# A chunked RWKV-7 recurrence: the chain of states taken one head at a time, or both heads of a pair in one step

## The chip, the core and the metric

The kernel runs on one core of a Trainium2 chip. Its engines work from queues of their own and wait for each other by semaphores: TensorE (PE: matmuls, and PEld, the loading of their weights), VectorE (DVE), ScalarE (ACT), GpSimd (POOL) and SyncE (SP, which starts the DMAs). The metric is the device time of one execution in microseconds (us); less is better.

## The reference, cut to what matters

One decoder layer with 1024 tokens and 1024 channels: attention in three dilated groups, an RWKV-7 mixer with 16 heads of 64 channels, gates that merge the two, an output product and a squared-ReLU MLP. All is float32. The change touches the recurrence of the mixer:

```python
def step(state, inp):                       # per head; state is 64 x 64
    r_t, w_t, k_t, v_t, a_t, b_t = inp
    sa = jnp.einsum('bhvk,bhk->bhv', state, a_t)
    state = (state * w_t[:, :, None, :] + sa[..., None] * b_t[:, :, None, :]
             + v_t[..., None] * k_t[:, :, None, :])
    return state, jnp.einsum('bhvk,bhk->bhv', state, r_t)
_, ys = lax.scan(step, s0, xs)              # over 1024 tokens, from a zero state
```

## The kernel before

The kernel does not scan over tokens. It takes the 16 heads as eight pairs (m = 0 to 7; the heads of a pair lie on partitions 0 to 63 and 64 to 127) and each head's 1024 tokens as 16 chunks of 64. Within a chunk everything is matrix algebra; from chunk to chunk a 64 x 64 state is handed on. For each pair these steps run, each a function: P projects r, k and v out of the hidden rows (`project`, L307: 48 matmuls of 128 x 512 for each of the three, with operands split in a high and a low part); E and F make decays and features (`pair_lora`, `pair_features`, VectorE lines L649 to L709); g forms the products of the features within each chunk, the gram (`pair_gram`: PE L749 in groups of four chunks, each read out by VectorE at L755 and L757); V prepares the values (`pair_values`: PE L722, copies at L726); I inverts 32 unit triangles at once on VectorE (`pair_inverse`: 60 operations at L775 and L777 between two pairs of transposes, L769 and L781); L builds from all this one 128 x 128 matrix for each chunk and head (`pair_local`: PE L816, L820, L838, L853, with ScalarE copies at L817 and L854 and VectorE work at L845, L855 and L858), left in the tiles `fe`; C runs the chain (`pair_chain`); N normalizes (`pair_norm`), and G are gate projections (again L307).

The chain has 16 steps. The tile `sv` holds for each chunk a 128 x 64 operand: rows 0 to 63 are the chunk's values, rows 64 to 127 the state that enters it. PE multiplies it with the chunk's matrix in `fe` (L874); rows 0 to 63 of the product are the chunk's output, rows 64 to 127 the state that leaves it, which VectorE takes out of PSUM, scales by the decay `dd` (one number per row and chunk) and writes into the next chunk's `sv` (L877). Before, each head has its own `sv` tiles and its own PSUM bank (`ch0`, `ch1`, from the pool psC with one buffer each) for eight chunks; after eight chunks ScalarE copies the outputs into `y` (L880), and the next eight chunks use the same two banks. pair_norm uses the banks of psC too (L900, L911).

The string ORDER names the order in which the steps are written: "... P3 G2 C2 E3 F3 N2 g3 I3 V3 L3 P4 G3 C3 ...", so the chain of one pair stands beside projections and features of the next. The instructions are then laid by a scheduler, which takes for each engine what its own prices say is ready first, in the order of writing; the dense matmuls of P and G fill PE where the rest waits. Each engine then works in exactly that order. The gates G7 to G15 stand behind the last chain. The pool psS gives the gram, the values and the local steps two PSUM banks in all, so that each group of the gram (two banks) waits until VectorE has emptied the group ahead of it.

Of the kernel before, what the change touches and what calls it, by code (L numbers as in the profile page):

```python
# [8 lines left out]
F32 = mybir.dt.float32  # L9
# [4 lines left out]
OP = mybir.AluOpType  # L14
# [35 lines left out]
class Block:  # L50
# [608 lines left out]
    def pair_features(self, st, pr, m):  # L659

        nc = self.nc
        f4, b8 = st["f4"], st["b8"]
# [5 lines left out]
        ch = lambda ap: ap.rearrange("p (c t) -> p c t", t=64)  # L668
        ar = b8.tile([128, 2, S], F32, name="ar", bufs=1)
        bk = b8.tile([128, 16, 2, 64], F32, name="b8")  # L670
        dd = f4.tile([128, 2, 16], F32, name="dd", bufs=2)
        sv = [[f4.tile([128, 8, 64], F32, name="sv", bufs=6) for b in range(2)] for h in range(2)]
        pr.update(ar=ar, bk=bk, dd=dd, sv=sv)
        ar4 = ar.rearrange("p a (f c t) -> p (a f) c t", f=2, t=32)
        pr["ar4"] = ar4
# [3 lines left out]
        for i, hs in enumerate(halves):  # L679
            n = bk[:, 8 * i:8 * i + 8, 1, :]  # L680
            nc.scalar.activation(n, ch(k[:, hs]), AF.Square, scale=C("k_k"))
            p = pn[:, hs]
# [5 lines left out]
        for i, hs in enumerate(halves):  # L688
            c8 = slice(8 * i, 8 * i + 8)
# [21 lines left out]
    def pair_values(self, st, pr, m):  # L711


        nc = self.nc
# [3 lines left out]
        for i in range(2):  # L718
            hs = slice(512 * i, 512 * i + 512)
            pv = psS.tile([128, 4, 128], F32, name="s")  # L720
            for q in range(4):
                nc.tensor.matmul(pv[:, q, :], v[:, 512 * i + 128 * q:512 * i + 128 * q + 128], self.center,  # L722
                                 start=True, stop=True)
            for h in range(2):
                for e in range(2):
                    nc.scalar.copy(sv[h][i][0:64, e:8:2, :], pv[64 * e:64 * e + 64, :, 64 * h:64 * h + 64])  # L726
            nc.gpsimd.tensor_tensor(r[:, hs], r[:, hs], k[:, hs], OP.mult)
            p = psS.tile([128, 512], F32, name="s")
            nc.tensor.matmul(p, brk, r[:, hs], start=True, stop=True)
# [131 lines left out]
    def pair_chain(self, st, pr, m):  # L861

        nc = self.nc
        f4 = st["f4"]
        fe, sv, dd = pr["fe"], pr["sv"], pr["dd"]
        y = f4.tile([128, 16, 64], F32, name="lt", bufs=NLT)
        for h in range(2):
            nc.gpsimd.memset(sv[h][0][64:128, 0, :], 0.0)
        for b in range(2):
            ps = [st["psC"].tile([128, 8, 64], F32, name=f"ch{h}") for h in range(2)]  # L870
            for c8 in range(8):
                c = 8 * b + c8
                for h in range(2):
                    nc.tensor.matmul(ps[h][:, c8, :], fe[b][:, h, c8, :], sv[h][b][:, c8, :],  # L874
                                     start=True, stop=True)
                    if c < 15:
                        nc.vector.tensor_scalar(sv[h][(c + 1) // 8][64:128, (c + 1) % 8, :], ps[h][64:128, c8, :],  # L877
                                                dd[64:128, h, c:c + 1], None, op0=OP.mult)
            for h in range(2):
                nc.scalar.copy(y[64 * h:64 * h + 64, 8 * b:8 * b + 8, :], ps[h][0:64])  # L880
        pr["y"] = y

    def pair_norm(self, st, pr, m):
# [528 lines left out]
```

## Time and profile before

| | before |
|---|---|
| median of 3 runs | 2275.87 us (2270.26 to 2278.08) |
| the profiled execution | 2280.91 us |
| its span in the trace | 2279.2 us |
| PE busy | 2090.6 us, 92%, 10002 instructions |
| VectorE busy | 1567.8 us, 69%, 2845 instructions |
| ScalarE busy | 1036.3 us, 45%, 2018 instructions |
| GpSimd busy | 621.9 us, 27%, 461 instructions |

The span is what the trace covers, the execution's own time a little more. A share of busy time is a mean over all stages: attention comes first, the recurrence stands between about 430 and 1340 us, then come the gates, the merge, the output product and the MLP. The profile's chain of the work that ended last covers the later stages, so the recurrence has to be read from the busy time in stretches and from the waits. Where two records of one engine overlap, their durations add to more than its busy time. Times in views are microseconds from the start of the span, unless a duration is marked ns.

### The profile page before, as it was taken

The numbers are of one execution on the slowest core, as the hardware profiler recorded it, in microseconds if no ns is written. First come the engines' busy times: TensorE is split into PE (matmuls) and PEld (weight loads), VectorE is DVE, ScalarE is ACT, GpSimd is POOL, SyncE is SP. The second block draws the span as 40 slices with busy tenths as digits, with TensorE's granted clock in tenths as the row PEclk, the third lists the DMA queues.
The fourth block names the chain that finished last, engine by engine and source line by source line (L and its number), as shares of the span: only waits on it lengthen the run. The fifth ranks groups of instructions, "written<-read, shape, count | busy, mean of one in ns | idle before, by whom it ended". The sixth has DMA issues, their size and how long they took to land. (4 is left out here: it accounts for less than half of the span.)

```text
span 2279.2 us, 28241 instructions
## 1 busy us (share of the span) xinstructions
PE 2090.6 (92%) x10002; PEld 1628.6 (71%) x10002; DVE 1567.8 (69%) x2845; ACT 1036.3 (45%) x2018; POOL 621.9 (27%) x461
## 2 busy tenths in 40 slices
PE   6798999988989989898989999998699999999997
PEld 3676676666777767677777778876467777788876
DVE  5845555468879787867877744428766553799997
ACT  5534433345454635444645442126545443533332
POOL 2504310321213131222222133201000000988860
PEclk9999999999999999998998999999899999999998
DMA  7513311100011110101010164323354333433222
GB/s 257 169 31 102 98 38 33 56 28 24 25 33 37 31 34 29 34 29 34 24 48 31 54 202 144 125 93 118 118 168 161 116 106 125 155 128 114 93 102 74
DMA packets 156315, 194.88 MB, mean 86 GB/s; under 512 B 10729, under 2 KB 110211, under 8 KB 154127
## 3 DMA queue, kind: packets, MB, share of 16 engines
q1 hardware_dynamic: 156175, 193.08, 25.5%
q8 instruction: 79, 1.29, 0.2%
q14 instruction: 61, 0.50, 0.1%
HBM read 152.14 MB, written 40.90 MB: 85 GB/s over the span
## 5 line engine op out<-in xcount | busy, mean ns | idle before, releaser
L307 PE MATMUL d<-hh,w_h 128*128 128x512 f32 x960 | 329.0, 415 | 7.2 <-ACT w_h L64 4.0
L307 PE MATMUL d<-hl,w_h 128*128 128x512 f32 x960 | 331.1, 415 | 2.9 <-DVE hl L280 2.9
L307 PE MATMUL d<-hh,w_l 128*128 128x512 f32 x960 | 324.8, 410 | 2.6 <-DVE w_l L65 2.6
L1108 PE MATMUL m<-op 128*128 128x512 f32 x1272 | 295.8, 394 | 11.5 <-POOL op L65 6.4
L65 POOL TENSOR_TENSOR w_l<-w_t,w_h 128x256 fp32r<-128x256 f32 x160 | 129.3, 810 | 633.6 <-PE d L307 293.4
L1108 PEld LDWEIGHTS m<-op 128*128 128x128 f32 x1272 | 240.0, 190 | 66.9 <-POOL op L65 10.6
L1108 PE MATMUL m<-big,op 128*128 128x512 f32 x1152 | 275.1, 399 | 5.1 <-ACT op L64 2.1
L1108 PEld LDWEIGHTS m<-big,op 128*128 128x128 f32 x1152 | 212.8, 188 | 67.3 <-DVE u L1220 4.2
L64 ACT CAST w_h<-w_t 128x256 fp32r<-128x256 f32 x272 | 108.7, 404 | 316.4 <-PE d L307 230.7
L307 PEld LDWEIGHTS d<-hl,w_h 128*128 128x128 f32 x960 | 181.5, 193 | 45.5 <-issue 10.1
L307 PEld LDWEIGHTS d<-hh,w_h 128*128 128x128 f32 x960 | 180.8, 193 | 46.3 <-issue 5.7
L307 PEld LDWEIGHTS d<-hh,w_l 128*128 128x128 f32 x960 | 181.1, 192 | 44.0 <-issue 8.5
L64 ACT CAST op<-t 128x512 fp32r<-128x512 f32 (+1 forms) x152 | 114.2, 776 | 182.8 <-PE m L1108 121.5
L65 DVE TENSOR_TENSOR op<-t,op 128x512 fp32r<-128x512 f32 (+1 forms) x124 | 118.5, 975 | 28.0 <-ACT op L64 27.8
L153 POOL TENSOR_TENSOR macc<-macc,ada_t 128x512 f32<-128x512 f32 x56 | 87.5, 1564 | 181.3 <-ACT macc L151 162.7
L1266 POOL TENSOR_TENSOR t<-big 128x1024 f32<-128x1024 f32 x7 | 16.9, 2410 | 352.1 <-DMA big<-in_w_ff_dram 331.3
L1282 DVE TENSOR_TENSOR big<-big,m 128x1024 f32<-128x1024 f32 x88 | 104.4, 1210 | 3.8 <-PE m L1108 3.8
L775 DVE TENSOR_TENSOR lt<-lt 64x30 f32<-64x30 f32 (+14 forms) x240 | 96.9, 404 | 8.2
L777 DVE TENSOR_TENSOR lt<-lt 64x30 f32<-64x30 f32 (+14 forms) x240 | 94.2, 392 | 7.7
L874 PEld LDWEIGHTS ch<-sv,fe 128*128 128x128 f32 x512 | 83.3, 191 | 20.3 <-DVE sv L877 8.9
L65 DVE TENSOR_TENSOR w_l<-w_t,w_h 128x256 fp32r<-128x256 f32 x112 | 61.6, 555 | 48.6 <-ACT w_h L64 34.9
L65 POOL TENSOR_TENSOR op<-t,op 128x1024 fp32r<-128x1024 f32 x28 | 93.2, 3339 | 4.3 <-ACT op L64 4.3
(379 smaller groups left out, 3925.8 us busy)
## 6 DMA issues: line engine op xcount, KB each, us to landing
w_t<-in_w_in_dram SPq DMA_DIRECT2D x240, 128.0 KB
ada_t<-in_ada_w_dram SPq DMA_DIRECT2D x64, 256.0 KB
fS<-ft SPq DMA_DIRECT2D x64, 256.0 KB
t<-in_w_ff_dram SPq DMA_DIRECT2D x16, 1024.0 KB
big<-fS SPq DMA_DIRECT2D x16, 1024.0 KB
big<-in_w_ff_dram SPq DMA_DIRECT2D x16, 1024.0 KB
x<-in_x_dram SPq DMA_DIRECT2D x16, 512.0 KB
ada_t<-in_ada_w_dram SPq DMA_DIRECT2D x16, 512.0 KB
```

Source lines behind the costliest of these rows:

```text
L64: nc.scalar.copy(hi, t)
L65: (eng or nc.vector).tensor_tensor(lo, t, hi.bitcast(F32), OP.subtract)
L153: nc.gpsimd.tensor_tensor(acc, acc, t, OP.add)
L307: nc.tensor.matmul(p[:, 512 * half + cs.start:512 * half + cs.stop], a, b[half][k][:, cs], start=k == ks[0] and i == 0, stop=k == ks[-1] a ...
L775: nc.vector.tensor_tensor(q, lb[:, s + 1:32, s:s + 1].to_broadcast([64, n, s]), lb[:, s:s + 1, 0:s].to_broadcast([64, n, s]), OP.mult)
L777: nc.vector.tensor_tensor(lb[:, s + 1:32, 0:s], lb[:, s + 1:32, 0:s], q, OP.add)
L874: nc.tensor.matmul(ps[h][:, c8, :], fe[b][:, h, c8, :], sv[h][b][:, c8, :], start=True, stop=True)
L1108: self.nc.tensor.matmul(p, s, m, start=start and k == 0 and i == 0, stop=k == len(a) - 1 and i == 2, skip_group_check=not start)
L1266: vb.tensor_tensor(sb[:, 0], wr[:, k1, h2], wr[:, k1, h1], OP.subtract)
L1282: nc.vector.tensor_tensor(acc[nm][h], acc[nm][h], ps2[h], OP.add)
```

## The change

Both heads of a pair go through the chain together. One `sv` tile holds both heads for eight chunks. The 16 steps are cut in four quarters; a quarter has one PSUM bank, in which the two heads' products of a chunk lie side by side, and the quarters use the banks `ch0` and `ch1` in turn. VectorE takes both states in one tensor_tensor of 64 partitions by 2 by 64 elements, whose second operand is `dd` read with a step of zero over the 64 columns. The copies into `sv` (pair_values) become two for each half, with 512 elements, the copies into `y` two for each quarter, with 256 elements.

```diff
-        sv = [[f4.tile([128, 8, 64], F32, name="sv", bufs=6) for b in range(2)] for h in range(2)]
+        sv = [f4.tile([128, 2, 8, 64], F32, name="sv", bufs=3) for b in range(2)]
...
-            for h in range(2):
-                for e in range(2):
-                    nc.scalar.copy(sv[h][i][0:64, e:8:2, :], pv[64 * e:64 * e + 64, :, 64 * h:64 * h + 64])
+            for e in range(2):
+                nc.scalar.copy(sv[i][0:64, :, e:8:2, :],
+                               pv[64 * e:64 * e + 64].rearrange("p q (h t) -> p h q t", h=2))
...
-        for h in range(2):
-            nc.gpsimd.memset(sv[h][0][64:128, 0, :], 0.0)
-        for b in range(2):
-            ps = [st["psC"].tile([128, 8, 64], F32, name=f"ch{h}") for h in range(2)]
-            for c8 in range(8):
-                c = 8 * b + c8
+        nc.gpsimd.memset(sv[0][64:128, :, 0, :], 0.0)
+        for q in range(4):
+            ps = st["psC"].tile([128, 4, 2, 64], F32, name=f"ch{q % 2}")
+            for i in range(4):
+                c = 4 * q + i
                 for h in range(2):
-                    nc.tensor.matmul(ps[h][:, c8, :], fe[b][:, h, c8, :], sv[h][b][:, c8, :],
+                    nc.tensor.matmul(ps[:, i, h, :], fe[c // 8][:, h, c % 8, :], sv[c // 8][:, h, c % 8, :],
                                      start=True, stop=True)
-                    if c < 15:
-                        nc.vector.tensor_scalar(sv[h][(c + 1) // 8][64:128, (c + 1) % 8, :], ps[h][64:128, c8, :],
-                                                dd[64:128, h, c:c + 1], None, op0=OP.mult)
+                if c < 15:
+                    nc.vector.tensor_tensor(sv[(c + 1) // 8][64:128, :, (c + 1) % 8, :], ps[64:128, i],
+                                            dd[64:128, :, c:c + 1].to_broadcast([64, 2, 64]), OP.mult)
             for h in range(2):
-                nc.scalar.copy(y[64 * h:64 * h + 64, 8 * b:8 * b + 8, :], ps[h][0:64])
+                nc.scalar.copy(y[64 * h:64 * h + 64, 4 * q:4 * q + 4, :], ps[0:64, :, h, :])
```

The scheduler lays all engines anew. On VectorE, in the chain of pair 1, `sv` are the states (L877, now L876), the other rows the features of pair 2. Before:

```order
L705 TENSOR_TENSOR b8_5612<-rkv_5346,ft_5593 128x8x64
L877 TENSOR_SCALAR sv_4741<-ch0_5507,dd_4739 64x64
L877 TENSOR_SCALAR sv_4743<-ch1_5508,dd_4739 64x64
L707 COPY dd_5613<-ft_5630 64x8 x2
L708 TENSOR_TENSOR ar_5611<-ft_5628,ft_5630 128x2x256
L709 TENSOR_TENSOR ar_5611<-rkv_5270,ft_5630 128x2x256
L877 TENSOR_SCALAR sv_4741<-ch0_5543,dd_4739 64x64
L877 TENSOR_SCALAR sv_4743<-ch1_5544,dd_4739 64x64
L694 SCALAR_TENSOR_TENSOR ft_5644<-rkv_5346,col_166,b8_5612 128x512
```

and now, at the seam of two quarters:

```order
L709 TENSOR_TENSOR ar_5575<-rkv_5246,ft_5608 128x2x256
L876 TENSOR_TENSOR sv_4723<-ch0_5512,dd_4721 64x2x64
L755 TENSOR_TENSOR b8_5667<-s_5670,gmask_160 128x4x2x32
L757 TENSOR_TENSOR fe_5668<-s_5670,gmask_160 128x4x64
L876 TENSOR_TENSOR sv_4723<-ch1_5527,dd_4721 64x2x64
L755 TENSOR_TENSOR b8_5667<-s_5671,gmask_160 128x4x2x32
L757 TENSOR_TENSOR fe_5668<-s_5671,gmask_160 128x4x64
```

Where two updates stood between pieces of the features there is one, and the readings of the next gram (L755, L757) have come into the chain.

On PE, at the end of the same chain (products L874, now L873), L307 are dense matmuls that fill, and L749 are products of the next pair's gram. Before:

```order
L874 MATMUL ch_5544<-sv,fe 128x64
L307 MATMUL d<-hh,w_l 128x512
L307 MATMUL d<-hh,w_h 128x512 x2
L307 MATMUL d<-hl,w_h 128x512 x2
L749 MATMUL s<-ar,b_5612 128x128 x8
L307 MATMUL d<-hh,w_l 128x512 x2
```

and now:

```order
L873 MATMUL ch_5527<-sv,fe 128x64 x2
L749 MATMUL s<-ar,b_5576 128x128 x7
L307 MATMUL d<-hh,w_h 128x512
L749 MATMUL s<-ar,b_5576 128x128 x4
L307 MATMUL d<-hl,w_h 128x512 x2
L307 MATMUL d<-hh,w_l 128x512 x2
```

A group of eight gram products stood behind the chain with five dense matmuls between; now seven products of the gram follow the chain's last step at once, and most of the others stand ahead of it. From the chain's end to the eight L816 of this pair PE has 112 dense matmuls in place of 106 and 15 gram products in place of 24.

On PE behind the chain of a later pair the gram stays whole. In pair 4, before:

```order
L874 MATMUL ch_8166<-sv,fe 128x64
L307 MATMUL d<-hh,w_l 128x512
L307 MATMUL d<-hh,w_h 128x512 x2
L307 MATMUL d<-hl,w_h 128x512 x2
L307 MATMUL d<-hh,w_l 128x512
L749 MATMUL s<-ar,b_8234 128x128 x8
```

and now, in pair 5:

```order
L873 MATMUL ch_8951<-sv,fe 128x64 x2
L307 MATMUL d<-hl,w_h 128x512
L307 MATMUL d<-hh,w_l 128x512 x2
L307 MATMUL d<-hh,w_h 128x512 x2
L749 MATMUL s<-ar,b_9000 128x128 x8
L307 MATMUL d<-hl,w_h 128x512 x2
```

From the first group of eight to the second there are 20 dense matmuls in the one and 21 in the other. In the order before this is so in pairs 2, 4 and 6, in the new one in pairs 3 and 5; in pairs 2, 4 and 6 the new order has one group of eight inside the chain and 19 dense matmuls from the chain's end to the next group.

## Rows read from the trace of the kernel before

**Rows 1.** Stretch, length, busy us of PE, PEld, DVE, ACT, POOL (count); clock, DMA, GB/s.

```profile
538.52:645.67 107.15, 96.07 (x502) 76.49 (x502) 86.89 (x191) 53.85 (x113) 23.07 (x27) 0.91 0.08 25
645.67:742.59 96.92, 87.05 (x493) 69.49 (x493) 82.52 (x187) 53.60 (x110) 22.31 (x28) 0.98 0.10 31
742.59:854.14 111.55, 100.56 (x531) 79.51 (x531) 87.85 (x193) 55.14 (x113) 25.32 (x31) 0.94 0.11 33
854.14:953.82 99.68, 90.20 (x499) 71.21 (x499) 84.35 (x187) 53.66 (x110) 22.85 (x28) 0.96 0.10 32
953.82:1069.86 116.04, 106.30 (x533) 85.11 (x533) 87.11 (x194) 55.53 (x114) 25.06 (x31) 0.88 0.10 32
1069.86:1169.57 99.71, 89.46 (x499) 71.49 (x499) 83.83 (x187) 53.77 (x110) 22.67 (x28) 0.96 0.10 32
1169.57:1278.69 109.12, 99.83 (x517) 80.02 (x517) 83.98 (x188) 53.99 (x114) 24.52 (x29) 0.89 0.14 45
1336.20:1544.80 208.60, 207.08 (x909) 169.85 (x907) 80.49 (x88) 58.19 (x98) 46.02 (x31) 1.00 0.43 137
```

**Rows 2.** Waits of PE, 560 to 1340 us: us in total, times, longest.

```profile
PE s L816 <- ACT lt L817: 31.5, 7, 5.2
PE s L749 <- DVE fe L757: 7.5, 3, 2.5
...
PE ch L874 <- DVE sv L877: 1.5, 4, 0.4
```

**Rows 3.** VectorE in order of time: start, us, line, operation, tiles, shapes, count.

```profile
679.82 0.50 DVE L877 TENSOR_SCALAR sv<-ch,dd 64x64 f32<-64x64 f32 x2
680.34 0.69 DVE L704 SCALAR_TENSOR_TENSOR b<-ft 128x512 f32<-128x512 f32 x1
```

**Rows 4.** PE in order of time, chain and gram (a product shows two records).

```profile
678.79 0.63 PE L307 MATMUL d<-hh,w_l 128*128 128x512 f32 x2
679.25 0.55 PE L874 MATMUL ch<-sv,fe 128*128 128x64 f32 x4
...
680.62 0.55 PE L874 MATMUL ch<-sv,fe 128*128 128x64 f32 x4
...
682.00 0.55 PE L874 MATMUL ch<-sv,fe 128*128 128x64 f32 x4
...
683.83 0.33 PE L874 MATMUL ch<-sv,fe 128*128 128x64 f32 x2
...
696.04 1.71 PE L749 MATMUL s<-ar,b 64*128 64x128 f32 x16
```

**Rows 5.** Groups by line and shape, 560 to 1270 us: busy us, mean ns; idle before.

```profile
L877 DVE TENSOR_SCALAR sv<-ch,dd 64x64 f32<-64x64 f32 x210 | 55.1, 289 | 17.1 <-PE ch L874 14.0
...
L755 DVE TENSOR_TENSOR b<-s,gmask 128x256 f32<-128x256 f32 x56 | 24.4, 435 | 31.2 <-PE s L749 30.8
...
L757 DVE TENSOR_TENSOR fe<-s,gmask 128x256 f32<-128x256 f32 x56 | 23.3, 416 | 0.1
...
L726 ACT COPY sv<-s 64x256 f32<-64x256 f32 x56 | 20.6, 368 | 6.4 <-PE s L722 5.9
...
L880 ACT COPY lt<-ch 64x512 f32<-64x512 f32 x28 | 16.2, 577 | 15.8 <-PE ch L874 10.9 <-DVE sv L877 4.6
...
L709 DVE TENSOR_TENSOR ar<-rkv,ft 128x512 f32<-128x512 f32 x14 | 10.4, 744 | 0.2
...
L840 DVE TENSOR_TENSOR lt<-lt,s 128x512 f32<-128x512 f32 x12 | 8.2, 686 | 3.7 <-PE s L838 3.5
```

**Rows 6.** PE in order of time, at the gram of the fifth period.

```profile
1009.88 0.39 PE L307 MATMUL d<-hh,w_h 128*128 128x512 f32 x1
1012.79 1.13 PE L749 MATMUL s<-ar,b 64*128 64x128 f32 x8 [2.52 <-DVE fe L757]
```

**Rows 7.** Two stretches with a gram, columns as in rows 1.

```profile
900.00:917.00 17.00, 15.97 (x103) 12.94 (x103) 15.68 (x42) 6.48 (x14) 6.64 (x6) 1.00 0.09 25
1012.00:1036.00 24.00, 22.26 (x79) 17.19 (x80) 13.13 (x32) 7.06 (x15) 7.25 (x6) 0.57 0.04 12
```

## The prediction

> **What bounds the kernel now.** I read the stretches first. One period of the recurrence stage, from the end of one pair's triangular inverse on VectorE to the end of the next one's, takes 97 to 116 us [rows 1]. In it the reader should see that no engine is full: PE is busy 87 to 106 us, VectorE 82 to 88 us. PE's idle part is nearly the same in all seven periods: 107.15 - 96.07 = 11.1 us in the first, then 9.9, 11.0, 9.5, 9.7, 10.3 and 9.3 us, together 70.7 us. What differs is the clock: 0.98 in the shortest period, 0.88 in the longest. [...] Behind the stage stands a stretch in which PE is busy 207.08 of 208.60 us at clock 1.00 (the last row of [rows 1]): the gate projections that nothing holds up. So a microsecond that PE loses less in the stage is a microsecond off the end, and matmuls that only change sides cost nothing. [...]
>
> Next the waits of PE [rows 2]. The chain itself hardly holds PE: 1.5 us in all. The largest wait is that of the eight transposes at L816 for the ScalarE copy at L817, 31.5 us over seven, so 4.5 us a pair; L817 waits for the inverse on VectorE, which runs without a gap up to it. The second is the gram at L749, which waits for VectorE to empty a bank (L757): 7.5 us, three times. PE therefore waits for VectorE's queue, not for the chain's latency. VectorE carries the 30 chain operations of a pair in front of both places.
>
> **The change part by part.** *VectorE, 30 operations a pair become 15.* In the trace two L877 in a row take 0.50 us, and the next operation starts 0.52 us after the first [rows 3]; alone one takes 0.289 us [rows 5]. The combined operation, 64 partitions by 128 elements out of PSUM with a second tensor from SBUF, is not in the trace. The nearest are the tensor_tensor of 256 elements out of PSUM (L755, L757, 0.416 and 0.435 us) and of 512 (L840, 0.686 us) [rows 5]: about 1.0 ns an element between them, so an estimate of 0.30 us at 128. Bounds: not below one L877, 0.29 us; at most the price at 256 elements, 0.43 us. With the same 0.03 us behind it a step costs 0.33 us in place of 0.52: 0.19 us by 15 steps is 2.9 us a pair, 23 us over eight. At the dear end it is 0.06 by 120, 7 us. I take 0.30, because the two neighbours lie on a line and the operand read by broadcast is no longer than the mask that L757 reads by broadcast.
>
> The rows price a 64-element operation out of PSUM at 0.289 us and a 256-element one at 0.42 to 0.44 us [rows 5]. [...]
>
> *PE, the same 32 products a pair.* Tiles, shapes and weights are the same; only the bank and the order differ; of the dense matmuls 706 in place of 690 stand behind the last chain, 3.6 us that leave the stage and come back after it. In the trace a step's two products stand behind four dense matmuls, and steps start 1.37 us apart (679.25, 680.62, 682.00), the first two rows giving 0.23 us for a dense matmul [rows 4]. Cost 0.
>
> *The chain's latency.* Before, head 0's update runs while PE does head 1's product; now one update waits for both. A step from rows: two products of 0.23 us each, 0.30 us of VectorE, two hand-overs of about 0.1 us, 0.95 to 1.0 us. The dense matmuls between steps hide that: three or four stand there (0.7 to 0.9 us on top of the 0.46 us of products). Where nothing stands between, in the new order only at a run of six products in pairs 3 and 5, PE idles 0.5 us a step, twice per pair: 2 us in all.
>
> *Banks.* With one bank a head, step 8 had to wait for the copies at L880: it starts 1.83 us after step 7 [rows 4], 0.46 us more than the others. With four banks' worth of steps in two alternating banks a copy has a whole quarter of the chain. That saves at most 0.46 by 8, 3.7 us, and it was covered by dense matmuls, so I book 0.
>
> *ScalarE and GpSimd.* The result copies go from 4 of 512 elements to 8 of 256: 8 by 0.368 - 4 by 0.577, +0.64 us; the value copies go the other way, -0.64 us [rows 5]. Nothing; ScalarE is busy half of a period [rows 1]. Two memsets become one. No DMA and no queue of SP changes.
>
> *What arrives at PE's waits.* The scheduler lays the work anew, so I counted the two orders from the last chain step of a pair to the eight L816, each row at its mean duration. Pair 1 in full: VectorE has 3 L755, 3 L757 and one L709 fewer there, 3 by 0.435 + 3 by 0.416 + 0.744 = 3.3 us, the rest is the same work [rows 5]; PE has nine gram products fewer (a run of eight takes 1.71 us [rows 4], so 1.9 us) and six dense matmuls more (1.4 us), 0.5 us less. VectorE's lead over PE, which is the wait, shrinks by some 2.9 us, from 7.0 to 4.0. The same count for pairs 0 to 6 gives a VectorE excess of 7.0, 7.0, 8.3, 7.0, 8.3, 7.0, 7.4 us before and 4.1, 4.0, 5.8, 7.8, 5.8, 7.8, 6.2 us after: 52 against 41.5, so 10.5 us less idle. Pairs 3 and 5 get worse, since there the chain now ends before the features' second half. PE's own wait for the chain, 1.5 us [rows 2], goes as well, since PE's rows outweigh VectorE's there in the new order. Together 12 us.
>
> *The clock.* PE lost 52 us to the lower clock with 70.7 us of idle time, 0.74 us per microsecond [rows 1]. I carry that ratio: 12 by 1.74 is 20.9 us. With the 2 us of bare steps the **sum is -19 us**. The profiled execution took 2280.91 us, which makes 2262; it lies 5 us above the median of the runs, 2275.87, so for the median **2257 us**. Bounds: without the clock's share 12 - 2 = 10 us, 2266; with all of VectorE's 23 us arriving and the clock's share, 23 by 1.74 = 40 us, 2236; at VectorE's dear end 7 by 1.74 - 2 = 10 us, 2266 again.
>
> **The rivals.** *The whole relief arrives* (2236 us). For it: VectorE is gapless for most of the stretch before L816. It needs pairs 3 and 5 not to lose what the others win, and the gram's stall not to come back. That stall is the trace's clearest slip: in the fifth period PE runs out of dense matmuls at 1010.3 us, waits 2.52 us for L757 [rows 6], and the next 24 us go at clock 0.57, where the same place one period earlier went at 1.00 [rows 7]. Against it: the new order keeps that gap in pairs 3 and 5.
>
> *No difference* (2276 us, 2269 to 2283). The orders are laid by a planner with its own prices. PE waits at L816 because VectorE is later than planned; the chain's saving was planned with, so fewer dense matmuls stand in the chain (43 in place of 53 in pair 1) and the same lateness returns at L816. For it: PE's idle part is 9.3 to 11.1 us in every period, whatever the order in it. The same time comes out if the combined operation costs what two did. Against it: the count above shows a lead shrinking in five of seven pairs.
>
> *Slower, by the gram's slip* (2291 us). Periods with the slip average (111.55 + 116.04 + 109.12) / 3 = 112.2 us, the three without it 98.8 us [rows 1]; the counts of PE's rows differ by 6.8 us (90.1 against 83.3), so a slip costs 6.6 us. Before, it sits in pairs 2, 4 and 6. Counted from the chain's end to the second group of the gram, PE arrives there after 7.5 us and VectorE is done with the first group after 10.2; the new order has the same figures in pairs 3 and 5, and 4.3 against 5.7 us in pairs 2, 4 and 6. If these slip as well there are five in place of three, +13 us, and the bare steps +2, with the relief eaten up at half clock. It decides where PE's wait at that place passes from tenths of a microsecond to over 2 us.
>
> **How the numbers follow.** Forecast 0.48, whole relief 0.17, no difference 0.20, slower 0.15. A measurement of this kernel can tell about 0.3%, 7 us, from no change. Both faster cases lie below 2269: faster 0.65, within 0.20, slower 0.15. The forecast's own range is 2236 to 2268; the range for 8 in 10 reaches from 2234 into the slower case, to 2284, which leaves out some 0.05 below and 0.1 above.
>
> **What would show it.** 120 operations of 64 by 128 elements at 0.29 to 0.33 us (0.43 or more would make it the second rival); VectorE's busy time in a period down by about 3 us; the wait L816 for L817 down from 4.5 to about 3 us a pair, but not in pairs 3 and 5; PE's idle part per period 8 to 9 us; clock 1.00 at the gram of pairs 2, 4 and 6 and below 0.8 at that of 3 and 5. The forecast is wrong if PE's idle part stays at 10 us, if waits for the chain's update (L873 for L876) grow beyond some 5 us, or if the stretch behind the stage stops being full of PE work.

## The result, and the profile after

The changed kernel takes 2294.1 us (median of 4 runs) against 2275.9 us: a ratio of 1.0081, 95% interval 1.0056 to 1.0107. It is **slower** by 0.8%, where 0.8% faster was forecast, and it lies outside the range. The profiled execution took 2289.69 us with a span of 2288.0 us.

First the seven periods and the stretch behind the stage, cut as in [rows 1] (stretch, length, busy us of PE, PEld, DVE, ACT, POOL, clock, DMA, GB/s):

```profile
537.16:639.60 102.44, 90.25 (x499) 71.44 (x499) 80.88 (x177) 53.85 (x112) 22.36 (x25) 0.95 0.09 26
639.60:740.72 101.12, 89.26 (x492) 70.75 (x492) 80.37 (x173) 53.28 (x109) 23.36 (x26) 0.96 0.10 30
740.72:845.15 104.43, 94.05 (x512) 74.12 (x512) 83.08 (x176) 53.92 (x111) 22.30 (x27) 0.97 0.10 32
845.15:958.69 113.54, 101.12 (x519) 78.61 (x519) 83.50 (x176) 55.16 (x113) 24.62 (x29) 0.91 0.10 31
958.69:1065.60 106.91, 96.40 (x513) 74.92 (x513) 83.69 (x175) 54.19 (x112) 22.33 (x27) 0.95 0.10 31
1065.60:1180.15 114.55, 101.65 (x519) 79.17 (x519) 83.48 (x176) 55.14 (x113) 24.62 (x29) 0.89 0.10 31
1180.15:1285.69 105.54, 96.02 (x500) 75.30 (x500) 80.35 (x174) 53.33 (x112) 22.19 (x26) 0.90 0.12 41
1343.80:1552.40 208.60, 207.06 (x909) 170.05 (x909) 79.07 (x83) 58.31 (x97) 45.94 (x32) 1.00 0.43 138
```

See three things. The stretch behind the stage is as full of PE work as before, so what PE loses in the stage still moves the end. VectorE is busy 575.4 us in the seven periods, against 596.5: the 21 us that the change was to save are saved. And PE's idle part is larger all the same: 79.8 us against 70.7. The clock's loss, estimated as (1 - clock) times the length and summed over the seven periods, is 51 us, against 52 from [rows 1]. The fourth and the sixth period, which hold the chains of pairs 3 and 5, went from 99.7 us each to 113.5 and 114.6; the second grew by 4.2 us, and the first, third, fifth and seventh together went from 443.9 to 419.3. Not all of this is loss, since dense matmuls moved between the periods (519 PE records in place of 499 in the fourth and the sixth, 512 and 513 in place of 531 and 533 in the third and the fifth); idle time and the clock's loss together rose by some 20 us in the fourth and sixth and fell by some 12 in the other five.

The waits of PE, 560 to 1340 us (us, times, longest), to hold against [rows 2]:

```profile
PE s L816 <- ACT lt L817: 37.9, 7, 5.7
PE s L749 <- DVE fe L757: 9.3, 9, 2.6
PE ch L899 <- POOL lt L893: 7.2, 6, 1.8
PE ch L873 <- DVE sv L876: 5.1, 12, 0.6
```

The large wait rose by 6.4 us where it was to fall by 10, and the wait for the chain's operation, 1.5 us before, is 5.1. The combined operation itself, by line and shape over 560 to 1270 us (busy us, mean ns, idle before), cost what was estimated:

```profile
L876 DVE TENSOR_TENSOR sv<-ch,dd 64x128 f32<-64x128 f32 x105 | 30.9, 295 | 25.7 <-PE ch L873 23.2
```

0.295 us for 128 elements out of PSUM, where one head's 64 took 0.289 [rows 5].

What happens in the fourth period is seen in order of time (start, us; idle before). The chain of pair 3 now begins when nearly all of its own local work is done and the dense matmuls have run out:

```profile
875.26 0.66 PE L873 MATMUL ch<-sv,fe 128*128 128x64 f32 x4 [0.39 <-DVE sv L876]
875.95 0.29 DVE L876 TENSOR_TENSOR sv<-ch,dd 64x128 f32<-64x128 f32 x1 [0.75 <-PE ch L873]
...
876.30 0.66 PE L873 MATMUL ch<-sv,fe 128*128 128x64 f32 x4 [0.39 <-DVE sv L876]
...
877.00 0.29 DVE L876 TENSOR_TENSOR sv<-ch,dd 64x128 f32<-64x128 f32 x1 [0.75 <-PE ch L873]
...
878.07 1.11 PE L873 MATMUL ch<-sv,fe 128*128 128x64 f32 x4
...
878.94 0.77 PE L645 MATMUL d<-dws,lorah 128*128 128x512 f32 x1
...
879.65 0.79 PE L646 MATMUL d<-dws,loral 64*128 64x512 f32 x1
...
880.37 1.11 PE L873 MATMUL ch<-sv,fe 128*128 128x64 f32 x4
...
904.76 0.39 PE L307 MATMUL d<-hh,w_l 128*128 128x512 f32 x1
...
907.77 4.23 PE L749 MATMUL s<-ar,b 64*128 64x128 f32 x16 [2.62 <-DVE fe L757]
```

A step takes 1.05 us (875.26 to 876.30) with both engines waiting for each other in it. From 878 on the same products take 1.11 us in place of 0.66: the granted clock, 1.00 from 873 to 876 us, is 0.50 from 878 to 886. A step with two products of the lora step in it (L645, L646) takes 2.3 us there. At 907.77 the gram has its slip (PE waits for VectorE to empty a bank), as in the periods of [rows 6] before. Two stretches of this period, the bare part of the chain and the gram, show the clock (0.74 in both):

```profile
873.00:893.00 20.00, 19.23 (x77) 13.29 (x75) 10.02 (x23) 12.75 (x21) 0.79 (x2) 0.74 0.09 33
904.00:917.00 13.00, 10.20 (x46) 7.87 (x45) 10.16 (x28) 1.57 (x3) 4.11 (x5) 0.74 0.05 15
```

### The profile page after: what moved, and what is told of

Read it like the earlier page. It is cut to its first block, busy times and chain, and to the rows that moved or that the text cites. A ratio compares the mean times of both kernels' runs of the same rounds, so it can differ in the third digit from the quotient of the medians.

```text
span 2288.0 us, 28138 instructions
## 1 busy us (share of the span) xinstructions
PE 2094.2 (92%) x10002; PEld 1623.3 (71%) x10002; DVE 1522.1 (67%) x2725; ACT 1037.9 (45%) x2018; POOL 617.9 (27%) x453
## 5 line engine op out<-in xcount | busy, mean ns | idle before, releaser
L307 PE MATMUL d<-hh,w_h 128*128 128x512 f32 x960 | 324.9, 411 | 7.3 <-ACT w_h L64 4.0
L307 PE MATMUL d<-hh,w_l 128*128 128x512 f32 x960 | 323.2, 410 | 3.6 <-DVE w_l L65 3.6
L307 PE MATMUL d<-hl,w_h 128*128 128x512 f32 x960 | 320.4, 408 | 0.0
L307 PEld LDWEIGHTS d<-hh,w_h 128*128 128x128 f32 x960 | 181.1, 193 | 45.7 <-ACT w_h L64 4.8
L307 PEld LDWEIGHTS d<-hh,w_l 128*128 128x128 f32 x960 | 180.9, 192 | 45.7 <-issue 7.6
L307 PEld LDWEIGHTS d<-hl,w_h 128*128 128x128 f32 x960 | 180.1, 191 | 40.5 <-issue 7.4
L64 ACT CAST op<-t 128x512 fp32r<-128x512 f32 (+1 forms) x152 | 113.7, 776 | 172.1 <-PE m L1107 119.6
L775 DVE TENSOR_TENSOR lt<-lt 64x30 f32<-64x30 f32 (+14 forms) x240 | 94.6, 394 | 13.2 <-PE ch L899 2.7
L873 PEld LDWEIGHTS ch<-sv,fe 128*128 128x128 f32 x512 | 74.7, 199 | 28.8 <-DVE sv L876 14.1
L65 DVE TENSOR_TENSOR w_l<-w_t,w_h 128x256 fp32r<-128x256 f32 x112 | 56.3, 506 | 53.6 <-ACT w_h L64 42.4
```

The costliest lines, as they stand in the source:

```text
L64: nc.scalar.copy(hi, t)
L65: (eng or nc.vector).tensor_tensor(lo, t, hi.bitcast(F32), OP.subtract)
L307: nc.tensor.matmul(p[:, 512 * half + cs.start:512 * half + cs.stop], a, b[half][k][:, cs], start=k == ks[0] and i == 0, stop=k == ks[-1] a ...
L775: nc.vector.tensor_tensor(q, lb[:, s + 1:32, s:s + 1].to_broadcast([64, n, s]), lb[:, s:s + 1, 0:s].to_broadcast([64, n, s]), OP.mult)
L873: nc.tensor.matmul(ps[:, i, h, :], fe[c // 8][:, h, c % 8, :], sv[c // 8][:, h, c % 8, :], start=True, stop=True)
```

## The experiments

Two kernels that differ in one operation are laid in two different orders by the planner, so a comparison holds little unless the order is held. Kernel 1 is the kernel of run 1, and so on. Most of them therefore carry a table of the wanted order, engine by engine, and edges that only order (no wait is added between engines):

```diff
+def pin(tc, nc):
...
+    info = mybir.DependencyInfo(mybir.DependencyClass.NoSync, mybir.DependencyReason.SCHED_ONLY)
+    for e, t in TABLE.items():
+        o = array.array("H", zlib.decompress(base64.b85decode(t)))
+        for a, b in zip(o, o[1:]):
+            tc.add_manual_dep(at[e][b], at[e][a].name, info, reason="order")
...
         Block(tc, aps, out).build()
+        pin(tc, nc)
```

All ratios are to the kernel before, on the same chip, with 95% intervals.

### 1 and 2: the instructions of the one in the order of the other

Edit of 1: `pin` with the order of the kernel before, on the changed kernel. Edit of 2: `pin` with the changed kernel's order, on the kernel before.

> All the instructions of the changed kernel, but on each engine in the order of the kernel before: the planner's choice is overruled by edges that only order, the combined operation stands where the second head's operation stood, and 32 of the 64 copies of the chain's results on ScalarE, which have no counterpart, are left to the planner. Nothing is left out of the computation. Theory O (the combined operation and the shared bank cost nothing, the loss is the planner's new order): 2250 to 2266 us, 10 to 26 us under the kernel before (120 operations of 0.29 us fewer is 35 us, 120 x (2 x 0.289 - 0.295) = 34 us of VectorE time at most, 23 by the plain count of busy time after), and the changed kernel's extra idle of TensorE in pairs 3 and 5 gone. Rival L (in lockstep each step has to wait for both products, and that latency is on the path): 2280 to 2300 us in any order, TensorE waiting for the combined operation well over 5 us more than in the kernel before. Rival B (one bank for both heads, four banks in place of two, copies cut otherwise): 2280 to 2300 us too, and then the third run of this call shows it without the combined operation.

> All the instructions of the kernel before, but on each engine in the order of the changed kernel: the two operations of a step stand together where the combined one stood; 64 value copies, 32 result copies on ScalarE and 16 memsets on GpSimd, which have no counterpart, are left to the planner. Nothing is left out of the computation. Theory O: no faster than the changed kernel, 2292 to 2318 us: the stretches of pairs 3 and 5 are as long as there or longer (113 us against 99.7 before), since 23 us of VectorE time come back and the chain is as bare. Rivals L and B: the separate operations and banks bring the time back to that of the kernel before, 2270 to 2282 us.

Measured: 2298.8 us, 1.0107 (1.0080 to 1.0135), and 2303.4 us, 1.0126 (1.0101 to 1.0152). The second is as theory O has it: with not one operation changed, the new order costs 1.3%, and its fourth and sixth period are 115.2 and 113.7 us long, as in the changed kernel. Part of it may be kernel 2's own: PE waits 5.3 us there for ScalarE's copy L880 out of the two banks, a wait that neither the kernel before nor the changed kernel shows. So whether the combined operation gives anything back in that order (the changed kernel, 1.0081) is not shown; the two intervals overlap as well. But the first speaks against theory O: the order of before with the combined operation is as bad. PE's waits in it, 560 to 1340 us:

```profile
PE s L816 <- ACT lt L817: 31.4, 7, 5.3
PE ch L873 <- DVE sv L876: 13.2, 31, 1.1
```

The largest wait is that of [rows 2]. New is that PE stands 31 times at a product whose state isn't there.

### 3 and 4: the shared bank with two operations, and a third order

Edit of 3, on the changed kernel, with `pin` to the order of before:

```diff
-                if c < 15:
-                    nc.vector.tensor_tensor(sv[(c + 1) // 8][64:128, :, (c + 1) % 8, :], ps[64:128, i],
-                                            dd[64:128, :, c:c + 1].to_broadcast([64, 2, 64]), OP.mult)
+                    if c < 15:
+                        nc.vector.tensor_scalar(sv[(c + 1) // 8][64:128, h, (c + 1) % 8, :], ps[64:128, i, h, :],
+                                                dd[64:128, h, c:c + 1], None, op0=OP.mult)
```

Edit of 4: the changed kernel, `pin` with the order that the planner makes of kernel 3 when nothing is pinned.

> The changed kernel's tiles (both heads in one tile of states, one PSUM bank a quarter for both heads, its copies and memsets), but two separate operations a step, one a head, and on each engine the order of the kernel before. Nothing is left out of the computation. Theory O and rival L: as the kernel before, 2270 to 2282 us, VectorE's busy time 1567 us as before. Rival B: 2284 to 2300 us.

> The changed kernel's instructions in a third order: the one that the planner makes of the changed tiles with two operations a step. In it the chain of each of pairs 0 to 6 is written among the next pair's features and all four groups of its gram, so that no gram stands whole behind a chain. Nothing is left out of the computation. Theory O: the stretches of pairs 3 and 5 fall to 95 to 103 us from 113.5 and 114.5, no wait of TensorE for L757 over 1.5 us in pairs 2 to 6, and the time is 2240 to 2268 us. Rivals L and B: no better than the changed kernel, 2285 to 2305 us, since each step's latency stays.

Measured: 2366.5 us, 1.0412 (1.0386 to 1.0438), and 2339.7 us, 1.0279 (1.0253 to 1.0306). Kernel 3, PE's waits and then VectorE's, 560 to 1340 us:

```profile
PE ch L873 <- DVE sv L876: 43.2, 73, 2.3
```

```profile
DVE sv L876 <- PE ch L873: 79.2, 131, 1.6
```

What ran as two chains beside each other is one chain twice as long, and costs 92 us in this order: between 500 and 1290 us 74 of 210 operations overlap a product on PE in the kernel before, one of 206 here. The two heads share a tile of states and a bank. Kernel 7 below, with the shared tile and a bank for each head, has 75 such overlaps and no loss, so the bank is what is left. That is rival B's side, far above its range. Why the product of one head and the operation of the other take turns in the shared bank is not shown; that they do is in the waits above (43.2 us of PE for the operation, 79.2 of VectorE for the product). So the shared bank is not neutral: with the one operation it is free (kernel 5 below), with two in this order it is dear; two operations with the heads in step, as in kernel 6, were not run in it. Kernel 4, slower than any range given for it, refutes theory O's best case: a chain among the features and all of the gram is no remedy. VectorE waits 85.6 us for products there (19.8 before), and the wait at L816 is 53.7 us.

### 5 to 7: both products of a step together, and the tile of states

Edit of 5: kernel 1 with one change to PE's list, made at each of the 128 steps. In rows of PE:

```diff
-L873 MATMUL ch_4641<-sv,fe 128x64
-L307 MATMUL d<-hh,w_h 128x512
-L873 MATMUL ch_4641<-sv,fe 128x64
+L307 MATMUL d<-hh,w_h 128x512
+L873 MATMUL ch_4641<-sv,fe 128x64 x2
```

Edit of 6: the same move in the kernel before, on PE for the products and on VectorE for the two operations. Edit of 7, on the kernel before, nothing pinned: of the change only the one tile `sv` for both heads, with its copies and its one memset.

> As the first run of this study (the changed kernel's instructions in the order of the kernel before), with one difference: the first head's product of each step is moved down to stand directly ahead of the second head's, so that TensorE no longer comes early to a product whose state isn't there. Nothing is left out of the computation. In the first run TensorE waited 13.2 us for the combined operation (1.5 us for L877 in the kernel before) and VectorE 62.8 us for the products (19.8). Theory S (stagger: the two heads' chains of the kernel before run out of phase, so that one's product is made while VectorE updates the other; the combined operation puts them in phase, and the two engines wait for each other in turn): still 2275 to 2300 us, VectorE's wait for the products over 30 us. Rival P (only the early place of the first head's product costs): 2250 to 2270 us, TensorE's wait for the operation under 4 us and VectorE's for the products about 20 us.

> The kernel before with its two operations a step and its two banks, and with its own order but for the chain: both products of a step stand together in the place of the second, and both operations in the place of the second. Nothing is left out of the computation. It has the phase of the combined operation without the operation. Theory S: 2285 to 2310 us, VectorE's wait for the products over 30 us (19.8 before). Rival P, and any theory in which the shared bank or the combined operation itself costs: 2270 to 2282 us.

> One part of the change alone: the states of both heads in one tile, with its half as many value copies of twice the size and its one memset; two banks, two operations a step, copies of the results as before. Nothing is left out of the computation. Theory S and rival P: as the kernel before, 2270 to 2282 us. Rival B (the tile of states or its copies cost): 2284 us or more.

Measured: 2275.8 us, 1.0003 (0.9985 to 1.0020); 2277.4 us, 0.9996 (0.9976 to 1.0015); 2275.8 us, 0.9997 (0.9977 to 1.0018). All three take the time of the kernel before. Theory S falls with kernel 6: putting the two heads in phase costs nothing. What was wrong in kernel 1 was the place of a product: one that stands too early in PE's list holds up the dense matmuls behind it (in kernel 1 for 13.2 us, 31 times). And kernel 5 has no loss left but no gain either: in the seven periods VectorE is busy 575.1 us against 595.0 in kernel 6, 20 us less in an order otherwise equal, and the time does not move. Rival P was right that the loss goes and wrong that a gain comes. PE's wait at L816 in kernel 5, and VectorE's wait for the chain's products in kernel 5 and in kernel 6, 560 to 1340 us:

```profile
PE s L816 <- ACT lt L817: 30.0, 7, 5.2
```

```profile
DVE sv L876 <- PE ch L873: 38.2, 60, 1.8
```

```profile
DVE sv L877 <- PE ch L874: 18.4, 31, 1.6
```

The 20 us are found again, whole, as VectorE's wait for the chain's products (theory S had this wait right, over 30 us, and its price wrong). PE, for its part, is idle for only 0.9 us in the 182 us of seven chains in kernel 5, 1.8 us in kernel 6. Two stretches of kernel 5's fourth period, the chain of pair 3 and most of the inverse behind the gram:

```profile
869.00:905.00 36.00, 35.03 (x224) 28.54 (x223) 29.93 (x70) 17.68 (x32) 9.30 (x10) 1.00 0.07 19
905.00:942.00 37.00, 33.55 (x163) 25.78 (x163) 33.82 (x75) 17.70 (x40) 12.48 (x13) 0.95 0.12 38
```

Kernel 6, the same two stretches:

```profile
869.00:905.00 36.00, 35.42 (x223) 28.66 (x223) 32.95 (x84) 18.26 (x30) 8.57 (x10) 1.00 0.07 20
905.00:942.00 37.00, 33.80 (x170) 25.42 (x168) 34.55 (x80) 18.20 (x44) 11.98 (x14) 1.00 0.12 38
```

In the first PE is busy 35 of 36 us in either, VectorE 29.93 us with the combined operation and 32.95 without. The saved 3 us of VectorE are there, as idle time, in a stretch that PE fills. The second stretch holds the inverse, which the change does not shorten, and PE waits for its end at L816 (at 946 us, 3.76 us in kernel 5 and 4.54 in kernel 6).

### 8, 15 and 16: where the chain is written

Edit of 8 (on the changed kernel) and of 15 (on the kernel before), for the chains of pairs 0 to 6:

```diff
-ORDER = "... P4 G3 C3 E4 F4 N3 g4 ..."
+ORDER = "... P4 G3 E4 C3 F4 N3 g4 ..."
```

Edit of 16, on the changed kernel: the chain's loop under `with self.tc.high_priority(offset=100):`.

> The changed kernel, planned anew with the chain of a pair written behind the next pair's lora step (E) in place of ahead of it; nothing else differs and nothing is left out of the computation. In the order that comes of it pairs 3 and 5 have the form that pairs 4 and 6 have in the changed kernel: feature and local operations stand among the steps there. If the bare chain of pairs 3 and 5 is what the changed kernel lost by (stretches of 113.6 and 114.5 us against 99.7 and 99.7): those stretches fall to 100 to 107 us and the time is 2265 to 2284 us. Theory S: the stretches fall, but the waits for the products stay over 30 us, and the time is 2278 to 2295 us.

> The kernel before (two operations a step, two banks), with the chain of a pair written behind the next pair's lora step as in the eighth run, planned anew. Nothing is left out of the computation. If that run won by the shape of pairs 3 and 5 alone, which the kernel before already had right: 2270 to 2285 us. If this way of writing is better for any kernel: 2258 to 2268 us, and the combined operation would lose 15 us and more against it.

> The changed kernel with the chain's products, operations and copies given 100 places more of priority in the planner, so that in pairs 3 to 6 the steps stand regularly among local and feature operations and the chain ends before the second half of the features. Nothing is left out of the computation. Theory R (time on VectorE counts only behind the gram): the chain's place is of no use in itself, and since feature operations move behind the chain, ahead of the gram, the gram comes later: 2280 to 2305 us. If a regular chain is what the combined operation needed: 2255 to 2272 us.

Measured: 2283.4 us, 1.0033 (1.0015 to 1.0051); 2278.8 us, 1.0015 (0.9995 to 1.0035); 2291.3 us, 1.0079 (1.0053 to 1.0104). The two long periods of kernel 8:

```profile
842.35:948.57 106.22, 94.45 (x513) 73.94 (x513) 83.39 (x176) 54.92 (x112) 24.81 (x28) 0.97 0.10 32
1056.84:1163.75 106.91, 95.87 (x516) 74.90 (x516) 83.64 (x176) 54.62 (x112) 23.77 (x28) 0.95 0.10 32
```

106 and 107 us in place of 114 and 115, clock 0.97 and 0.95 in place of 0.91 and 0.89: with this form of pairs 3 and 5 some 11 of the 18 us are gone. It takes away two things at once, and no run parts them. The chain is no longer bare; the same place as above (873 to 893 us there) goes at full clock:

```profile
870.00:890.00 20.00, 18.93 (x105) 14.16 (x104) 15.64 (x33) 15.31 (x25) 2.31 (x3) 1.00 0.07 25
```

And the gram's slip goes too:

```profile
PE s L749 <- DVE fe L757: 3.0, 6, 0.6
```

VectorE's wait for products is 23.4 us, under theory S's 30. Kernel 15 shows that the way of writing is worth nothing where the chain is not bare. Kernel 16 came out as theory R had it: a regular chain is no aim in itself. Kernel 8's wait at L816 is still 37.2 us.

### 9: the same time taken from VectorE behind the gram

```diff
-        for s in range(1, 31):
+        for s in (*range(1, 14), *range(19, 31)):
```

on the kernel before, with `pin` to its own order.

> The kernel before in its own order, with VectorE's work cut in another place: of the 30 steps of each pair's inverse (two operations each) steps 14 to 18 are left out, 10 operations of 0.38 to 0.40 us and the gaps between them, 4.3 us a pair and 34 us in all, which is what the combined operation takes off the chain (120 x (2 x 0.289 - 0.295) = 34 us). That part of the inverse isn't computed; all else is. Theory R (rendezvous: in the stretch of the chain TensorE is the limit and VectorE waits, so time saved there is lost again at the wait for the gram's products; after the gram the inverse on VectorE is the limit and TensorE waits for it at L816, so only time saved there counts): 2246 to 2262 us, TensorE's wait at L816 (31.5 us over the seven periods) down to under 15 us. Rival V (VectorE's time counts nowhere any more; what is lost at L816 is ScalarE's copies or the latency of semaphores): 2270 to 2282 us, the wait at L816 as it was.

Measured: 2250.0 us, 0.9891 (0.9864 to 0.9918). PE's wait at L816, and then the seven periods as one, first of this kernel and then of the kernel before:

```profile
PE s L816 <- ACT lt L817: 17.0, 6, 3.1
```

```profile
531.32:1244.36 713.04, 653.40 (x3557) 518.63 (x3558) 568.70 (x1257) 375.77 (x776) 165.13 (x196) 0.95 0.11 33
```

```profile
534.70:1274.86 740.16, 669.45 (x3574) 533.32 (x3574) 596.54 (x1326) 377.95 (x779) 165.66 (x197) 0.93 0.10 32
```

This is the counterpart of kernel 5: VectorE is busy 28 us less in the seven periods (568.70 against 596.54), taken from the inverse and not from the chain, and that is worth 26 us. (The edit leaves these steps out in all eight pairs.) PE idles 11 us less in the seven periods, and the rest is clock: 0.95 in place of 0.93. Theory R holds in its time; the wait at L816 fell by 14.5 us, to 17.0, and not under 15.

### 10 to 12: dense matmuls moved out of the chain's stretch

If PE fills the chain's stretch and idles at L816, dense products could change places. Edit: in PE's list, 16 dense products a period (19 to 23 in kernel 12) leave the gaps between steps and stand ahead of L816, as here in kernel 10:

```diff
+L307 MATMUL d<-hh,w_h 128x512 x2
+L307 MATMUL d<-hl,w_h 128x512 x2
 L307 MATMUL d<-hh,w_l 128x512 x2
 L816 MATMUL s<-ident,b_5667 128x128 x4
```

> The combined operation in the order of the kernel before with both products of a step together, as in the fifth run, and in each of the seven periods 16 places of dense products (L307, 0.227 us each, 3.6 us) taken out from between the steps of the chain and put directly ahead of the next pair's first L816, where TensorE waits. The dense products keep their order among themselves; their consumers (L542, L543, L606) and the splits of the weights (L64, L65) are left to the planner. Nothing is left out of the computation. Theory R: VectorE has 4.3 us a pair to spare in the chain now, so the chain and the gram come 2 to 3.6 us earlier and the places fill the wait at L816: 2250 to 2268 us, that wait under 20 us. Rival V: 2270 to 2285 us. If the steps of the chain are already bound by the way from product to operation and back, TensorE's wait for L876 rises by as much as the wait at L816 falls: 2272 to 2285 us.

> The same move of 16 dense products a period in the kernel before (two operations a step, two banks, products together as in the sixth run), so that it differs from the run above by the combined operation alone. Nothing is left out of the computation. Theory R: VectorE has less to spare in the chain (4.3 us a pair less), so it gains less or nothing: 2262 to 2280 us, 5 to 15 us over the run above. If the move gains by itself and the combined operation is worth nothing even so: equal to the run above within 4 us.

> As the tenth run with 19 to 23 places a period moved in place of 16 (about 5 us, more than the wait at L816 of 4.5 us). Nothing is left out of the computation. Theory R: no better than the tenth run by more than 5 us, since the wait at L816 is used up and the chain's steps have become as short as the way from product to operation and back allows: 2248 to 2272 us. Rival V: 2272 to 2290 us.

Measured: 2281.4 us, 1.0038 (1.0021 to 1.0055); 2294.2 us, 1.0082 (1.0057 to 1.0106); 2292.0 us, 1.0078 (1.0057 to 1.0099). No gain: theory R's times for these runs were wrong, kernels 11 and 12 are slower than any range given for them, and rival V's range holds kernel 10. In kernel 10 the wait at L816 did fall, and another came up behind it:

```profile
PE s L816 <- ACT lt L817: 14.2, 7, 2.5
PE s L820 <- ACT lt L817: 10.1, 8, 2.3
```

Where the rest is lost these runs don't show. One thing they do: with less PE work between the steps, the combined operation is worth 13 us (kernel 10 against 11, intervals just apart, as theory R expected of the pair), against nothing in kernel 5. PE's idle time in the seven chains is 9.1 us in kernel 10 and 13.2 in kernel 11, where it was 0.9 and 1.8 in kernels 5 and 6. This fits theory R's core, that VectorE's time in the chain has a price only as far as PE leaves that stretch unfilled; the 4 us of idle time between the two are a part of the 13.

### 13 and 14: the gram's second mask off VectorE

On the kernel before in its own order, and on kernel 5:

```diff
-                nc.vector.tensor_tensor(fe[b // 2][:, h, 4 * (b % 2):4 * (b % 2) + 4, 0:64], p[:, :, 64:128], gmR, OP.mult)
+                fm = fe[b // 2][:, h, 4 * (b % 2):4 * (b % 2) + 4, 0:64]
+                nc.scalar.copy(fm, p[:, :, 64:128])
+                nc.gpsimd.tensor_tensor(fm, fm, gmR, OP.mult)
```

> The kernel before in its own order, with the second mask product of the gram (L757, 64 operations of 0.416 us, 3.3 us a pair) taken off VectorE: ScalarE copies the block out of PSUM and GpSimd multiplies it by the mask in SBUF, both placed by the planner. Nothing is left out of the computation. Theory R: VectorE's inverse starts up to 3.3 us earlier in each period and the time falls by 0.8 of that, 18 us of 23, as in the ninth run (26 of 34): 2254 to 2266 us, the wait at L816 about 20 us. If ScalarE's queue (chain copies, casts that wait for dense products) holds the banks of the gram longer than VectorE did: 2276 to 2300 us, with TensorE waiting for these copies at L749 or L785.

> The same with the combined operation, both products of a step together, otherwise the order of the kernel before (as in the fifth run). Nothing is left out of the computation. Theory R: as the run above within 6 us, since in the chain's stretch TensorE stays the limit. If the combined operation is worth something once the stretch behind the gram is relieved: 8 to 20 us under the run above, 2238 to 2252 us.

Measured: 2289.1 us, 1.0066 (1.0045 to 1.0087), and 2280.4 us, 1.0024 (1.0007 to 1.0041). Of kernel 13 the second expectation came in. Kernel 14 lies 9 us under it (intervals just apart), more than theory R allowed, although PE fills the chain there as in kernel 5 (1.4 us idle in 182). Kernel 14 also has the products of a step together, which kernel 13 has not; what the 9 us come from is not shown, and it stands against theory R. ScalarE's waits in kernel 13:

```profile
ACT fe L758 <- DVE b L755: 45.6, 33, 3.2
```

The copy reads the bank that VectorE's L755 reads, waits for it, and so lets the bank go later than before; PE then waits for the copy, 9.6 us at L749 and 5.3 at the next transposes. The wait at L816 stayed (33.3 us). Whether the stretch behind the gram can be relieved with all work computed is therefore not shown. No version that computes everything beat the kernel before.

## Why the prediction was wrong, point by point

**What bounds the kernel.** Right. The stretch behind the stage stayed full, and PE's loss accounts for the time: in the profiled executions idle +9.1 us and clock -1, together +8, against a span longer by 8.8. (The medians differ by 18 us because the profiled execution of before lay 5 us above its median, that of after 4 below.) Two of the three signs that I had named for a wrong forecast came: PE's idle part is 11.4 us a period, not 8 to 9, and the wait for the chain's update is 5.1 us, just over 5.

**The combined operation.** Right: 0.30 us estimated, 0.295 measured; 20 us for seven pairs expected of VectorE's busy time, 21 measured.

**The lead at L816.** This step failed, and the sign with it: 12 us less idle were booked, 20.9 with the clock, and PE idles 9.1 us more. I counted both engines' rows from the last chain step to L816, as if they started there abreast, and booked L755, L757 and L709 that had moved ahead of the chain's end as relief. They meet later: VectorE cannot start the inverse before PE has made the gram. In the kernel before the last reading of the gram (L757) ends 0.8 to 1.1 us behind the gram's last product in each of the seven pairs, and the inverse starts at once; from there to its end it takes 36 to 40 us. Time saved ahead of that meeting becomes VectorE's wait in a stretch that PE fills; the inverse behind it is what PE waits for. Kernel 5 (nothing for 20 us of VectorE's busy time) and kernel 9 (26 us for 28) show the two sides. *Whole relief* went by the same road. Kernel 14, with 9 us from an unknown cause where PE fills the chain, does not fit.

**The wait's rise.** Why the wait at L816 grew, and did not only stay, is open. The rival *no difference* had it come back because fewer dense matmuls stand in the chain, and there are fewer (in the fourth and sixth period 28 in place of 52). But those that PE does from the gram's first product to the L816 that waits are as many as before: 122 in place of 123 in the fourth and sixth period, 133 in both in the first. The waits at the end of these three went from 3.75, 4.54 and 4.26 us to 5.68, 5.71 and 5.42. The gram's slip, which the fourth and sixth period have now, is not the reason either: kernel 8 is without it and waits 5.67 and 5.68 us there. The rise, 6.4 us in all, is about what kernel 8 still loses.

**The chain's latency.** The mechanism was right, its size was not. A bare step was put at 0.95 to 1.0 us and takes 1.05: 0.66 for the two products, where 0.46 was booked, 0.29 of VectorE, and 0.03 and 0.06 for the two hand-overs, booked at 0.1 each (after, 875.26 to 876.30 us). But I looked for it at one run of six products, where pairs 3 and 5 have eight steps with no dense matmul between, only products of the lora step, and I left out that the granted clock falls there (0.74 over 20 us, by the same estimate 5.2 us lost in pair 3 alone), where a step with two lora products takes 2.3 us. Booked: 2 us. By kernel 8: some 11, together with the gram's slip in these pairs.

**The gram's slip.** Counted rightly: pairs 3 and 5 took it (2.62 us of waiting, clock 0.74), pairs 2, 4 and 6 lost it, and the third and fifth period are 7 and 9 us shorter. So it was luck that the rival *slower* named a time, 2291 us, near the result: it had five slips, and there are two, one fewer than before, on top of two bare chains.

**Banks, copies, PE's products.** Zero was right for the tile of states and its copies (kernel 7). For the shared bank it is right only with the one operation (kernel 3). The order of PE's products, booked at 0, is not free: it is worth 23 us between kernels 1 and 5.

**The clock.** No row shows the 52 us: they are (1 - clock) times the length, summed over the periods of [rows 1], an estimate that takes PE to work in proportion to the granted clock. Nor did the 0.74 us worked out from them for each microsecond of idle time hold: the ratio of clock to idle loss is not constant. Taken at 1.74 us in all for each microsecond of idle time, it was some 2.4 in kernel 9 (11 us of idle time, 27 in all), and in the changed kernel 9.1 us more idle time went with 1 us less of clock loss.

**Chances.** Slower had 0.15. The planner's new order was one mishap among three; kernels 2 and 5 together show that it was the larger part of the change: 1.3% with no operation changed, part of it perhaps kernel 2's own, against nothing for the operation in a held order. Kernel 8 gets 11 of the 18 us back by another order; where the other 7 are lost is open.

## What to carry to other kernels

Before booking time saved on an engine, find the next point at which it meets the engine that sets the end, and ask which of the two arrives there late: here time saved on the one that waits was worth nothing (kernel 5), and time saved behind the meeting nearly all of itself (kernel 9). Where a planner lays the work, an edit is two changes, an operation and an order: hold the order to price the first, and run the old operations in the new order to price the second. Before two chains are put into one PSUM bank, count the operations of the one that overlap a product of the other: in kernel 3 they fell from 74 to one, at 92 us.

## What the runs showed of the hardware that was not expected

A chain run bare cost twice here, by its waits and by the clock: the same four records of products take 0.66 us at 876 us and 1.11 us at 878, where the granted clock is 0.50, after PE had had only the chain and lora products since 873 us. And sharing a bank between a product and an operation of two chains, which no row of before could show, cost 92 us in kernel 3, four times what the combined operation was to bring.
